# HGRN scan: q times f at the head, two more steps of projections behind the transposes, and the 16-token matmul behind the first level

## The chip, the cores and the metric

The kernel runs on one core of one Trainium2 chip. The metric is the device time of one execution in microseconds (us). A core has engines that each work through a queue of their own in order: PE (matmul, with PEld for its weight loads), VectorE (DVE), ScalarE (ACT), GpSimd (POOL), and SP, which here only issues transfers. They wait for each other through semaphores.

## The reference

The reference is one inference step of a hybrid decoder layer: a feed-forward half step, a mixer of two groups (HGRN2 with 4 heads of key and value size 128, and Mamba-2 with 8 heads of 64), one output projection, a second feed-forward half step and a norm. 1024 prompt tokens with 16 learned tokens ahead of them, and 8 single decoding tokens, share all weights. The part in question is the HGRN2 group. Per head, with f the forget gate, k = 1 - f, and a state S of 128x128:

```
S_t = diag(f_t) S_{t-1} + k_t v_t^T
o_t = S_t^T q_t
o   = rmsnorm_per_head(o) * hg_norm * silu(g)
```

Over a chunk of tokens this is computed as scores, decayed between the two positions, and a part from the state ahead of the chunk:

```
scores[t,s] = sum_k q[t,k] k[s,k] * prod_{s<j<=t} f[j,k]        (s <= t)
o[t]        = sum_s scores[t,s] v[s]  +  (q[t] * prod_{j<=t} f[j]) S_prev
```

## The kernel before

Tokens lie along the free dimension, channels on the 128 partitions; 1040 prompt tokens make 8 chunks of 128 and a rest of 16, and 8 decoding tokens stand behind them. The input projection is split in units of 128 output columns (q0, f0, v0, g0, q1, ... for the heads, z0 and z1 for the Mamba group), with three products for one fp32 product (`mm3`, L163 to L165, tiles `acc`).

*Projections as filling.* The class `Fill` is a generator over these units. One step, a call of `fill(1)`, is one `mm3`, three wide matmuls, and after eight steps a piece of 344 or 350 tokens is complete and is evacuated by ScalarE or VectorE (L1603, L1607 to L1610, L1561). The mixer's small matmuls wait for VectorE and ScalarE in many places, and `fill(n)` puts n steps of projection there. `fill.until(name)` runs steps until a unit is finished. The stock is fixed: steps taken earlier are missing later.

*Order.* In the mixer (in `body`) PE's order is that of the code, which a manual schedule keeps. The other engines, and the output projection that follows the mixer (`out_proj`, evacuated at L1850, weights split at L157 and L158), are put in order by a scheduler from its own estimates. A change of PE's order can so move rows on any engine, and matmuls of `out_proj` can stand ahead of the mixer's last ones.

*The scan* (`hgrn_scan`, once for each of the four heads; I call them first to fourth scan) goes like this. v is transposed on PE (L1650, L1653, L1654) and copied from PSUM by ScalarE (two copies L1651, then L1655, L1656, tiles `vt`, `vt8`, `vs8`). `fill(3)` follows. POOL zeroes `pp`, `p8` and `pd`; VectorE makes `qf` = q * f (L1686). PE makes the diagonal blocks k^T q of 32x32 (32 calls, 64 rows in the trace, L1696) and that of the last 16 tokens (L1697, into the bank `s8`). Then come seven levels of a tree, m = 1, 2, 4, ..., 64 (`LEVELS`): at each level 32 matmuls join the first half of every pair of m-token groups to the second (L1725 below m = 32, L1716 above), one more does it for the 16 tokens (L1737, into the same `s8`), VectorE scales the second halves of `qf` and the first halves of k by products of f (L1747, L1748), makes the next products of f (L1750), and copies the scores that count out of PSUM under a mask (L1700, L1701 for the diagonal, L1729, L1740 for a level). `fill(5)` closes each level. A level's matmuls read the `qf` and k that VectorE scaled in the level ahead. At m = 2 and m = 16 `samples` loads and advances four decoding states (L1669, L1670, L1673 to L1675). Banks of PSUM for all the mixer's small work come from one pool (`K.psm()`, tiles `mis`), and wide SBUF tiles from pools named by tag (`K.slot("s")`, `"u"`), so an allocation waits until the buffer's former readers are done.

*Around it.* `hgrn_out` squares the outputs, sums over channels on PE (L1828), takes the constant-scaled sums off PSUM (L1829) and calls `rstd_wide` for the inverse root: a table load and four activations on ScalarE (L199, L201), three wide operations on VectorE (L202, L203, L204), and then L1831. `ssm_norm` does the same for the Mamba group (L1576 to L1578, PE L1583, ScalarE L1584, `rstd_wide`, VectorE L1587 twice). `ssm_norm(0)` stands ahead of the second scan, `hgrn_out` of the second head ahead of the third, `ssm_norm(1)` behind the fourth. Three of the output projection's operands come back from DRAM (`split_spilled`, L2075 to L2077), one is split at the end of the block.

## Time and profile before

| | us |
|---|---|
| median of 3 runs | 1979.41 (1973.97, 1979.57, 1979.41) |
| profiled execution | 1973.32 |
| its span | 1971.5 |
| PE busy | 1923.6 |
| DVE busy | 1529.7 |
| ACT busy | 859.9 |
| first to fourth scan, start of the transposes | 917.58, 1009.04, 1063.05, 1130.80 |
| end of the last L1583 row | about 1181.4 |

Times within the trace are microseconds from the span's start. A row of the timeline has the start, the duration, the engine, the line, the operation, output and inputs by name, shapes and a count; in brackets stands the engine's idle time just before the row and what ended it. Matmuls overlap, so a row's duration is longer than the distance between two starts. In the list of waits a row names the engine and the waiting line, then what was waited for, the sum, the number of times and the longest. "issue" is a wait for nothing that the profile shows.

### The profile page before, as it was taken

To read this page: it belongs to the slowest core of one execution; us is meant where nothing else is said; L and a number is where in the kernel's file an instruction comes from. 1 tells how busy PE (TensorE), PEld (TensorE's weight loads), DVE (VectorE), ACT (ScalarE), POOL (GpSimd) and SP (SyncE) were. 2 spreads that over 40 slices of the span, in tenths; PEclk is the share of its full clock that TensorE was granted. 3 is DMA by queue.
4 is the path that set the end of the run, shared out by engine and by line. 5 is a ranking of instruction groups with operands and counts; after the bars stand their busy time and mean duration, and the time that the engine had idled before them with its cause. 6 is when DMAs were issued, how large, how long until landed. Compare 5 with 4: busy or idle time off the path is not lost.

```text
span 1971.5 us, 40943 instructions
## 1 busy us (share of the span) xinstructions
PE 1923.6 (98%) x16585; PEld 1885.4 (96%) x16585; DVE 1529.7 (78%) x2720; ACT 859.9 (44%) x1647; POOL 82.7 (4%) x135
## 2 busy tenths in 40 slices
PE   7999999999999999999999999999999999999997
PEld 6999999999999999998988989999999999999997
DVE  7788888888788776675755557888888888878973
ACT  7533232324534555465644535752332333354352
POOL 4000000000001310000000001200000000000000
PEclk9999999999999999999999999999999999999999
DMA  7233333335976632222522153224332333587851
GB/s 220 77 98 97 98 107 96 108 93 171 302 240 214 184 117 61 69 88 73 167 82 72 61 169 126 85 82 119 92 108 87 103 103 112 160 251 230 275 178 68
DMA packets 323877, 258.45 MB, mean 131 GB/s; under 512 B 17568, under 2 KB 299424, under 8 KB 323680
## 3 DMA queue, kind: packets, MB, share of 16 engines
q1 hardware_dynamic: 323448, 255.79, 42.1%
q8 instruction: 131, 2.15, 0.4%
q14 instruction: 58, 0.48, 0.1%
q0 software_dynamic: 224, 0.04, 0.0%
q10 hardware_dynamic: 16, 0.00, 0.0%
HBM read 190.79 MB, written 65.05 MB: 130 GB/s over the span
## 4 chain that ended last, share of the span: by engine, by line
PE 87%; DVE 7%; ACT 2%; DMA 2%; issue 1%; POOL 0%; SPq 0%; DVEq 0%; ACTq 0%; POOLq 0%
PE acc L163 26%; PE acc L165 26%; PE acc L164 26%; PE mis L163 1%; PE mis L165 1%; PE mis L164 1%; DVE u L352 1%; DMA s<-in_x_prompt_dram 1%; PE mis L1725 1%; PE mis L1449 0%; PE mis L1782 0%; DVE ws L466 0%; PE mis L1445 0%; DVE u L341 0%; DVE t L301 0%
## 5 line engine op out<-in xcount | busy, mean ns | idle before, releaser
L163 PE MATMUL acc<-u,ws 128*128 128x258 f32 (+3 forms) x4248 | 1242.9, 293 | 6.7 <-ACT t L674 1.7
L164 PE MATMUL acc<-u,ws 128*128 128x258 f32 (+3 forms) x4248 | 1232.1, 290 | 2.9 <-DVE u L352 2.7
L165 PE MATMUL acc<-u,ws 128*128 128x258 f32 (+3 forms) x4248 | 1231.1, 290 | 3.5 <-DVE ws L466 3.4
L163 PEld LDWEIGHTS acc<-u,ws 128*128 128x128 f32 x4248 | 803.9, 189 | 12.2 <-ACT t L674 2.1
L164 PEld LDWEIGHTS acc<-u,ws 128*128 128x128 f32 x4248 | 806.5, 190 | 5.8 <-DVE u L352 4.0
L165 PEld LDWEIGHTS acc<-u,ws 128*128 128x128 f32 x4248 | 803.6, 189 | 5.2 <-DVE ws L466 4.8
L466 DVE TENSOR_TENSOR ws<-r,ws 128x512 fp32r<-128x512 f32 x276 | 190.6, 691 | 75.0 <-ACT ws L462 74.9
L462 ACT CAST ws<-r 128x512 fp32r<-128x512 f32 x276 | 160.1, 614 | 13.3 <-ACT ws L462 7.8
L458 DVE TENSOR_TENSOR r<-r,r 128x512 f32<-128x512 f32 x176 | 121.5, 692 | 2.7 <-DMA r<-in_w_ffn_up_dram 1.2
L681 ACT ACTIVATE t<-t 128x516 f32<-128x516 f32 (+1 forms) x41 | 26.2, 639 | 212.9 <-DVE t L669 212.9
L712 ACT ACTIVATE t<-t 128x524 f32<-128x524 f32 (+1 forms) x47 | 29.9, 639 | 196.1 <-DVE t L669 196.1
L846 DVE TENSOR_TENSOR u<-u,u 128x1048 fp32r<-128x1048 f32 (+3 forms) x84 | 97.0, 1156 | 5.3 <-ACT u L842 4.5
L669 DVE TENSOR_TENSOR t<-t,u 128x524 f32<-128x524 f32 (+1 forms) x135 | 92.9, 697 | 2.8
L230 POOL TENSOR_TENSOR t<-t,t 128x262 f32<-128x262 f32 (+1 forms) x56 | 54.4, 981 | 823.6 <-ACT t L229 820.4
L158 DVE TENSOR_TENSOR ws<-r,ws 128x512 fp32r<-128x512 f32 x88 | 60.5, 698 | 36.0 <-ACT ws L157 35.6
L903 ACT CAST ws<-u 128x512 fp32r<-128x512 f32 (+1 forms) x72 | 42.2, 586 | 103.2 <-DVE u L898 100.2
L932 DVE SCALAR_TENSOR_TENSOR s<-acc,s 128x524 f32<-128x524 f32 (+3 forms) x88 | 54.6, 643 | 36.9 <-PE acc L165 36.5
L842 ACT CAST u<-u 128x1048 fp32r<-128x1048 f32 (+3 forms) x84 | 82.8, 988 | 0.0
L908 DVE TENSOR_TENSOR ws<-r,ws 128x512 fp32r<-128x512 f32 (+1 forms) x84 | 57.6, 693 | 22.3 <-ACT ws L903 22.2
L903 ACT CAST ws<-r 128x512 fp32r<-128x512 f32 (+1 forms) x84 | 47.9, 582 | 61.6 <-DVE r L898 37.0
L157 ACT CAST ws<-r 128x512 fp32r<-128x512 f32 x88 | 53.7, 618 | 35.6 <-PE acc L165 30.6
L908 DVE TENSOR_TENSOR ws<-u,ws 128x512 fp32r<-128x512 f32 (+1 forms) x72 | 47.4, 658 | 26.8 <-ACT ws L903 26.8
(417 smaller groups left out, 2297.9 us busy)
## 6 DMA issues: line engine op xcount, KB each, us to landing
r<-in_w_ffn_down_dram SPq DMA_DIRECT2D x128, 256.0 KB
hd<-s SPq DMA_DIRECT2D x93, 258.0 KB
r<-in_w_ffn_gate_dram SPq DMA_DIRECT2D x88, 256.0 KB
r<-in_w_ffn_up_dram SPq DMA_DIRECT2D x88, 256.0 KB
hd<-s SPq DMA_DIRECT2D x77, 262.0 KB
u<-hd SPq DMA_DIRECT2D x36, 516.0 KB
u<-hd SPq DMA_DIRECT2D x28, 524.0 KB
r<-in_w_in_dram SPq DMA_DIRECT2D x56, 256.0 KB
```

Of the source, the lines that this page charges most:

```text
L158: self.nc.vector.tensor_sub(lo, src, hi.bitcast(F32))
L163: mm(ps, whi, xhi, start=first, stop=False, skip_group_check=more)
L164: mm(ps, whi, xlo, start=False, stop=False, skip_group_check=more)
L165: mm(ps, wlo, xhi, start=False, stop=last, skip_group_check=more)
L458: self.K.nc.vector.tensor_tensor(self.raw[p], self.raw[x], self.raw[y], op)
L462: self.K.nc.scalar.copy(self.w[p][:, : self.n * P], self.raw[p])
L466: self.K.nc.vector.tensor_sub(t[:, 512 : 512 + w], self.raw[p], t[:, :w].bitcast(F32))
L669: nc.vector.tensor_mul(t, t if src is None else src, spread.lanes(i, cs))
L842: K.nc.scalar.copy(hi, lo.bitcast(F32))
L846: K.nc.vector.tensor_sub(lo, lo.bitcast(F32), hi.bitcast(F32))
L903: nc.scalar.copy(w[p, j, g][:, : n * P], src)
L908: nc.vector.tensor_sub(t[:, 512 : 512 + n * P], box[0], t[:, : n * P].bitcast(F32))
```

## The change

It has three parts, all in `hgrn_scan`:

- `qf` is allocated and made as the first thing in the function, ahead of the transposes (L1686 before, L1639 now).
- `fill(3)` behind the transposes becomes `fill(5)`: 15 wide matmuls, not 9.
- The bank `s8` is allocated, and the 16-token diagonal matmul is issued, behind the matmuls of the first level and not ahead of them (L1697 before, L1734 now).

```diff
     nc = K.nc
     q, f, kg, v = u["q"], u["f"], u["k"], u["v"]
+    qf = K.slot("s", w=TP)
+    nc.vector.tensor_mul(qf, q[:, :TP], f[:, :TP])
...
-    fill(3)
+    fill(5)
...
-    qf = K.slot("s", w=TP)
-    nc.vector.tensor_mul(qf, q[:, :TP], f[:, :TP])
...
-    s8 = K.psm()
     ps = K.psm()
     for c in range(8):
         for r in range(0, P, 32):
             cs = slice(P * c + r, P * c + r + 32)
             nc.tensor.matmul(ps[r : r + 32, 32 * c : 32 * c + 32], kg[:, cs], q[:, cs], start=True, stop=True)
-    nc.tensor.matmul(s8[:16, 64:80], kg[:, 1024:TP], q[:, 1024:TP], start=True, stop=True)
...
             copies.append(copy)
+        if li == 0:
+            s8 = K.psm()
+            nc.tensor.matmul(s8[:16, 64:80], kg[:, 1024:TP], q[:, 1024:TP], start=True, stop=True)
```

Line numbers shift by a few: L1650 to L1652 and L1651 to L1653 (transposes of v and their copies), L1696 to L1695 (diagonal), L1725 to L1722 and L1716 to L1713 (levels), L1700, L1701 to L1697, L1698, L1729 to L1726, L1673 to L1675; L1737, L1740, L1747, L1748 and L1750 keep theirs.

What it does to the order is seen at the start of the third scan. PE there, before: the last wide matmul behind the transposes, the diagonal blocks, the 16-token matmul, the first level, the next wide matmul. The semaphores waited for stand in brackets.

```order
L165 MATMUL acc_12682<-u_8461,ws_12433 128x344
L1696 MATMUL mis_12733<-u_11914,u_12032 32x32 [waits Activation_49]
L1696 MATMUL mis_12733<-u_11914,u_12032 32x32 x31
L1697 MATMUL mis_12732<-u_11914,u_12032 16x16 [waits DVE_49]
L1725 MATMUL mis_12767<-s_12728,u_12032 32x16 [waits DVE_49,Activation_49]
L1725 MATMUL mis_12767<-s_12728,u_12032 32x16 x31
L1737 MATMUL mis_12732<-s_12728,u_12032 16x8
L163 MATMUL acc_12682<-u_8462,ws_12433 128x344
```

And now:

```order
L165 MATMUL acc_12736<-u_8457,ws_12374 128x344
L1695 MATMUL mis_12746<-u_11914,u_12032 32x32 [waits Activation_49]
L1695 MATMUL mis_12746<-u_11914,u_12032 32x32 x31
L1722 MATMUL mis_12779<-s_12695,u_12032 32x16 [waits DVE_49,Activation_49]
L1722 MATMUL mis_12779<-s_12695,u_12032 32x16 x31
L1734 MATMUL mis_12812<-u_11914,u_12032 16x16 [waits Activation_49]
L1737 MATMUL mis_12812<-s_12695,u_12032 16x8
L163 MATMUL acc_12736<-u_8458,ws_12374 128x344
```

The 16-token matmul has moved behind the level, and it waits for ScalarE where it waited for VectorE. The wide matmuls belong to a later piece of the projection, since two more steps stand ahead. VectorE at the same place, before: the end of `hgrn_out`'s norm of the second head, with the product L1686 between L203 and L204.

```order
L202 TENSOR_TENSOR s_12633<-s_12633,s_12634 128x1032 [waits Activation_49]
L1700 COPY_PREDICATED t_12730<-mid,mis_12733 128x256 [waits PE_49,Pool_49]
L203 SCALAR_TENSOR_TENSOR s_12633<-s_12633,s_12634 128x1032 [waits DVE_49]
L1686 TENSOR_TENSOR s_12728<-u_11914,u_12031 128x1040 [waits Pool_49]
L204 SCALAR_TENSOR_TENSOR s_12634<-s_12633,s_12634 128x1032 [waits DVE_49]
L1747 TENSOR_TENSOR s_12728<-s_12728,u_12031 128x520 [waits DVE_49,PE_49]
L1831 TENSOR_TENSOR u_11403<-u_11403,s_12634 128x1032 [waits DVE_49]
L1748 TENSOR_TENSOR u_12032<-u_12032,u_12031 128x520
L1750 TENSOR_TENSOR s_12803<-u_12031 128x520
L1701 COPY_PREDICATED p_1598_12726<-mid,mis_12732 16x16 [waits Pool_49]
L1729 COPY_PREDICATED t_12730<-mask_8800,mis_12767 128x128
L1740 COPY_PREDICATED p_1598_12726<-mask_8800,mis_12732 16x8 [waits DVE_49]
```

And now:

```order
L1639 TENSOR_TENSOR s_12695<-u_11914,u_12031 128x1040
L1750 TENSOR_TENSOR s_12817<-u_12031 128x520
L202 TENSOR_TENSOR s_12639<-s_12639,s_12640 128x1032 [waits Activation_49]
L1697 COPY_PREDICATED t_12744<-mid,mis_12746 128x256 [waits PE_49,Pool_49]
L203 SCALAR_TENSOR_TENSOR s_12639<-s_12639,s_12640 128x1032 [waits DVE_49]
L1747 TENSOR_TENSOR s_12695<-s_12695,u_12031 128x520 [waits PE_49]
L204 SCALAR_TENSOR_TENSOR s_12640<-s_12639,s_12640 128x1032 [waits DVE_49]
L1748 TENSOR_TENSOR u_12032<-u_12032,u_12031 128x520
L1831 TENSOR_TENSOR u_11379<-u_11379,s_12640 128x1032 [waits DVE_49]
L1698 COPY_PREDICATED p_1600_12742<-mid,mis_12812 16x16 [waits Pool_49]
L1726 COPY_PREDICATED t_12744<-mask_8800,mis_12779 128x128
L1740 COPY_PREDICATED p_1600_12742<-mask_8800,mis_12812 16x8 [waits DVE_49]
```

The product and the first product of f (L1750) now stand ahead of L202, and L1748 ahead of L1831. On ScalarE the table load and one evacuation L1603, which stood between L201 and the two copies of v there, now stand ahead of L1829, so that the copies follow L201. In the second scan ScalarE's order is the same; on VectorE the product moves from behind L203 to ahead of L1578, and L1750 to between L203 and L204.

The second place is the end of the block, `ssm_norm(1)` behind the fourth scan. PE, before: the three matmuls L1583 in a row.

```order
L165 MATMUL acc_14071<-u_8463,ws_13454 128x344
L1583 MATMUL mis_14093<-s_14056,ones_83 128x344 [waits DVE_49]
L1583 MATMUL mis_14096<-s_14056,ones_83 128x344 [waits Activation_49]
L1583 MATMUL mis_14099<-s_14056,ones_83 128x344 [waits Activation_49]
L163 MATMUL acc_14071<-u_8464,ws_13454 128x344
```

And now, with tiles of `out_proj` (`acc_14200`, `acc_14214`) between them:

```order
L165 MATMUL acc_14097<-u_8457,ws_13449 128x344
L1583 MATMUL mis_14101<-s_14062,ones_83 128x344 [waits DVE_49]
L163 MATMUL acc_14200<-u_13513,ws_14192 128x258 [waits Activation_49]
...
L164 MATMUL acc_14200<-u_13925,ws_14197 128x258
L1583 MATMUL mis_14104<-s_14062,ones_83 128x344 [waits Activation_49]
L165 MATMUL acc_14200<-u_13924,ws_14197 128x258
L163 MATMUL acc_14200<-u_14143,ws_14197 128x258
L164 MATMUL acc_14200<-u_14144,ws_14197 128x258 [waits DVE_49]
L165 MATMUL acc_14200<-u_14143,ws_14197 128x258
L163 MATMUL acc_14214<-u_13513,ws_14192 128x258
L164 MATMUL acc_14214<-u_13514,ws_14192 128x258
L1583 MATMUL mis_14107<-s_14062,ones_83 128x344 [waits Activation_49]
L163 MATMUL acc_14097<-u_8458,ws_13449 128x344
```

Eight and six matmuls of `out_proj` stand between the three; in the order before its first one followed the first L1828, 28 rows later. From there on, and ahead of the first scan, the order is the same on every engine but for numbers.

## The prediction

> **What bounds the kernel now.** I read the page's busy line first.

> ```profile
> PE 1923.6 (98%) x16585; PEld 1885.4 (96%) x16585; DVE 1529.7 (78%) x2720; ACT 859.9 (44%) x1647; POOL 82.7 (4%) x135
> ```

> PE is busy for 98% of the span. The change takes no matmul away and adds none, so all it can win is time in which PE stands. The next view is that of PE's waits, from the first scan's transposes to behind the last `ssm_norm` (915 to 1205 us), the only stretch whose order changes.

> ```profile
> PE mis L1725 <- DVE s L1686: 3.5, 2, 2.1
> PE mis L1725 <- issue: 2.9, 2, 2.3
> PE mis L1583 <- ACT s L1584: 1.5, 2, 0.9
> PE mis L1697 <- ACT s L1651: 1.4, 1, 1.4
> PE mis L1725 <- DVE u L1748: 1.0, 2, 0.7
> PE mis L1697 <- DVE t L1700: 1.0, 1, 1.0
> PE mis L1737 <- DVE p L1740: 0.6, 1, 0.6
> ...
> ```

> These seven sum to 11.9 us. The waits on L1686 (qf) and the two of L1697 (5.9 us) lie in the second and third scan, and they are what the diff touches. The timeline of PE in the second scan shows their places: diagonal blocks, the 16-token matmul, the first level, wide products, the second level.

> ```profile
> 1011.67 0.76 PE L1696 MATMUL mis<-u,u 128*32 128x32 f32 x64
> 1013.88 0.21 PE L1697 MATMUL mis<-u,u 128*16 128x16 f32 x2 [1.45 <-ACT s L1651]
> 1015.42 1.05 PE L1725 MATMUL mis<-s,u 128*32 128x16 f32 x64 [1.32 <-DVE s L1686]
> ...
> 1019.62 0.33 PE L164 MATMUL acc<-u,ws 128*128 128x350 f32 x1
> 1019.79 0.32 PE L165 MATMUL acc<-u,ws 128*128 128x350 f32 x1
> 1020.44 0.73 PE L1725 MATMUL mis<-s,u 128*32 128x16 f32 x64 [0.32 <-DVE u L1748]
> 1021.81 0.21 PE L1737 MATMUL mis<-s,u 128*16 128x8 f32 x2 [0.64 <-DVE p L1740]
> ```

> **The two added steps.** A step is three wide matmuls, started 0.16 us apart (1019.62 to 1019.79), so two steps are six starts, 0.97 us. They come out of the same stock of projections, and the later `fill.until` finds them done. I take them as neutral in themselves: whatever stands behind them starts 0.97 us later in the scan, and 0.97 us less work is left for later. So a gain is the difference of two times at the end of a level, plus 0.97.

> **The second scan.** The timelines of VectorE and, in the last row, of ScalarE at the same place:

> ```profile
> 1011.62 1.23 DVE L202 TENSOR_TENSOR s<-s,s 128x1032 f32<-128x1032 f32 x1 [12.49 <-ACT s L201]
> ...
> 1014.04 1.23 DVE L1686 TENSOR_TENSOR s<-u,u 128x1040 f32<-128x1040 f32 x1
> 1015.19 1.23 DVE L204 SCALAR_TENSOR_TENSOR s<-s,s 128x1032 f32<-128x1032 f32 x1
> ...
> 1017.19 2.49 DVE L1587 SCALAR_TENSOR_TENSOR u<-u,col,s 128x1032 f32<-128x1032 f32 x2
> 1019.60 0.69 DVE L1748 TENSOR_TENSOR u<-u,u 128x520 f32<-128x520 f32 x1
> 1020.21 0.69 DVE L1750 TENSOR_TENSOR s<-u 128x520 f32<-128x520 f32 x1
> ...
> 1021.53 0.20 DVE L1740 COPY_PREDICATED p<-mask,mis 16x8 f32<-16x8 uint8 x1
> ```

> ```profile
> 1013.25 1.07 ACT L1651 COPY s<-mis 128x512 f32<-128x512 f32 x2
> ```

> The product now stands ahead of L202, where VectorE idles for 12.49 us (9.87 in the third scan), so its 1.23 us cost nothing; without that idle time they would delay L202 and all behind it. PE's diagonal starts at 1011.67 + 0.97 = 1012.64 and is done by 1013.4. The first level then needs only the first of the two copies of L1651, half of 1.07 us from 1013.25: about 1013.8. The 16-token matmul behind it needs the second copy, by then done. With 0.73 us of level and 15 wide matmuls (2.4 us) PE asks for the second level at about 1017.1. What is late next is the keys that L1748 scales. VectorE's queue up to there loses L1686 (1.15 from start to start) and takes in L1750 (0.61), which the new order puts ahead of L204: L1748 goes from 1019.60 to about 1018.85, with its end at 1019.5. PE waits 2.3 us there, counted to L1748's end. L1740 started 1.93 behind L1748, with L1750 (0.61) between them that now stands earlier: 1018.85 + 1.32, about 1020.2, done by 1020.35, and the level's last matmul (1021.81 before) starts then: 1.46 + 0.97 = 2.4 us won.

> What a wait costs beyond itself is seen in the stretches by time, whose columns are length, busy time of PE, PEld, DVE, ACT and POOL, then the granted clock.

> ```profile
> 929.90:933.30 3.40, 2.94 (x35) 2.91 (x36) 2.31 (x6) 1.59 (x5) 0.00 (x0) 0.50 0.64 178
> 1015.30:1018.70 3.40, 3.28 (x74) 3.28 (x75) 3.24 (x4) 0.60 (x1) 0.00 (x0) 0.50 0.35 87
> ...
> ```

> Behind the waits PE runs 3.4 us at clock 0.50. In the second scan the 15 wide matmuls then ended at 1019.79 + 0.16, 3.55 us after the level's end, where 2.4 would do: about 1.1 us. A standstill of 2.3 us may call the same, as the first scan's did (2.27 us, below). So 1.3 to 2.4; I take the middle, 1.85. [...]

> **The third scan**, from the timelines of PE, ScalarE and VectorE:

> ```profile
> 1065.64 0.76 PE L1696 MATMUL mis<-u,u 128*32 128x32 f32 x64
> ...
> 1069.74 0.94 PE L1725 MATMUL mis<-s,u 128*32 128x16 f32 x61 [2.15 <-DVE s L1686]
> ...
> 1074.96 0.17 PE L1737 MATMUL mis<-s,u 128*16 128x8 f32 x1
> ```

> ```profile
> 1064.38 1.33 ACT L201 ACTIVATE s<-s,lna 128x516 f32<-128x516 f32 x2
> ```

> ```profile
> 1065.74 1.23 DVE L202 TENSOR_TENSOR s<-s,s 128x1032 f32<-128x1032 f32 x1 [9.87 <-ACT s L201]
> ...
> 1071.45 1.23 DVE L1831 TENSOR_TENSOR u<-u,s 128x1032 f32<-128x1032 f32 x1
> ```

> Here the shifted end of a projection lets ScalarE evacuate it earlier, so both copies stand right behind L201: 1065.7 to 1066.8. The diagonal starts at 1066.6, the first level at about 1067.2 without a wait, the wide matmuls end at about 1070.4. VectorE does L202, L1697 behind the diagonal (an estimate of 0.3, as it is between L1740's 0.20 and L1750's 0.69), L203 (1.2), L1747 (0.6, its shape is that of L1748), L204 (1.2) and L1748 to about 1071.3, so the second level waits 0.9; L1831 (1.2) and three small copies (some 0.5, by L1740) stand ahead of its last matmul, which starts at about 1073.0, not 1074.96: 1.96 + 0.97 = 2.9. Two waits of about 1 us each may call the half clock, so 1.8 to 2.9, middle 2.35.

> **The first and the fourth scan** have no wait on the moved pieces; PE stands inside the 64 matmuls of a later level.

> ```profile
> 930.36 0.55 PE L1725 MATMUL mis<-s,u 128*32 128x16 f32 x25 [2.27 <-issue]
> ...
> 1144.65 0.38 PE L1725 MATMUL mis<-s,u 128*32 128x16 f32 x23 [0.72 <-DVE u L1748]
> 1145.67 0.52 PE L1725 MATMUL mis<-s,u 128*32 128x16 f32 x40 [0.65 <-issue]
> ```

> "Issue" means that nothing shown was waited for. In the DMA view of that standstill (927.8 to 930.4 us) the queue of instructions moves one block, among the loads of the data queue:

> ```profile
> q1 hardware_dynamic: 1171, 0.59, 82.8%
> q8 instruction: 1, 0.02, 2.7%
> ```

> I read it as PE waiting for its program. The first scan's loads are issued behind its copies, which don't move, while PE comes 0.97 later: between nothing and 0.97 us of the 2.27 go, if the block keeps its time; I take 0.5. For the fourth I take half of 0.72 + 0.65, 0.7, between 0 and 1.4. [...]

> **The tail.** The steps shift where `ssm_norm(1)` falls, and the new order puts 8 and 6 matmuls of `out_proj` between its three L1583. Rows of PE, then of ScalarE and VectorE:

> ```profile
> 1179.02 0.85 PE L1583 MATMUL mis<-s,ones 128*128 128x344 f32 x2 [0.91 <-ACT s L1584]
> 1180.50 0.85 PE L1583 MATMUL mis<-s,ones 128*128 128x344 f32 x2 [0.64 <-ACT s L1584]
> ```

> ```profile
> 1177.46 1.05 ACT L2076 CAST u<-u 128x1032 fp32r<-128x1032 f32 x1 [2.73 <-DMA u<-mspill]
> ```

> ```profile
> 1178.55 1.23 DVE L2077 TENSOR_TENSOR u<-u,u 128x1032 fp32r<-128x1032 f32 x1 [9.90 <-ACT u L2076]
> ```

> The 1.55 us of waits would be filled. But the eleventh of the 14 needs L2077, done at 1179.8, which hangs on a load that ScalarE already waits for, and the last L1828 will come before its L1829. Between nothing and 1.6; I take 0.8. The instructions that SP, POOL and the two other queues pass (weight loads one place earlier, some evacuations) I cost at nothing: PE's wait list shows none of them.

> **Sum.** 0.5 + 1.85 + 2.35 + 0.7 + 0.8 = 6.2 us. With the low ends (the first scan's block 0.5 later, so -0.5) 2.6, with the high ends 9.3. The profiled execution took 1973.32 us (span 1971.5 and 1.8 around it): 1967.1. The runs shown are at 1973.97, 1979.41 and 1979.57, so their median lies 6.1 above it. With the profiled one, the middle of four executions is 1976.7, and I subtract from that: 1970.5. A measurement tells about 0.3% from no change, 5.9 us, and the forecast stands just at that bound.

> **Rivals.** *All at the high end:* no half clock follows, the program comes in time, the tail fills: 9.3 us, 1967.4. For it speaks that the clock's stretches don't begin with a wait (929.9 lies inside one); against it that in both stretches shown a wait had just ended or was ending.
> *The wait only changes its name:* if VectorE's queue at the second level is longer than worked out, by the samples' products or a weight split, what L1686 gave back goes to L1748 and L1740: about 2 us in all, 1974.7. For it speaks that L1748 and L1740 already show 1.6 us of waits.
> *Slower: the program comes late.* The waits that go (5.9 us) are also time in which instructions arrive; diagonal, first level and 16-token matmul now follow each other without a pause, with loads beside them. Each standstill costs 2.27 and 1.1 of half clock, 3.4 us. Two undo the sum, and from four on (13.6 - 6.2 = 7.4 slower) the kernel is measurably slower, 1984. Against it: in the first and fourth scan these pieces already follow without a wait, and the stall came two levels later.

> **Chances.** Forecast 0.50, six tenths of it beyond 5.9 us (0.30 faster, 0.20 same); high end 0.15, faster; renamed 0.17, same; late program 0.18, slower. That is 0.45 faster, 0.37 same, 0.18 slower. The range reaches from the high end against the profiled execution (1973.3 - 9.3, rounded to 1963.5) to the upper run with nothing won and a little lost, 1981.

> **What would show it.** Rows of PE waiting for qf and for the 16-token matmul vanish; L1725's successor L1722 waits for L1748 about 2.3 us in the second scan and 0.9 in the third, and L1737 for L1740 about 1 in the third; L1583's waits go. Wrong I am if "issue" grows beyond 2.9 us, if clock 0.50 fills more stretches than before, or if PE stands at the first `out_proj` matmuls for the load of `mspill`.

## The result and the profile after

| | before | after |
|---|---|---|
| median of 22 runs each, us | 1979.39 (1973.78 to 1985.46) | 1971.87 (1969.89 to 1975.67) |
| ratio to before | | 0.997 [0.9963, 0.9978] |
| profiled execution, us | 1973.32 | 1971.54 |
| its span, us | 1971.5 | 1969.7 |

By the ratio the changed kernel is 5.9 us faster (4.4 to 7.3), just at the 0.3% that the prediction named as its bound; the two medians lie 7.5 us apart. The two profiled executions lie only 1.8 us apart, and why that is less is part of the answer. The busy line first.

```profile
PE 1926.6 (98%) x16585; PEld 1889.5 (96%) x16585; DVE 1531.6 (78%) x2720; ACT 861.8 (44%) x1648; POOL 81.8 (4%) x135
```

The number of matmuls is the same, and PE is still busy for 98%. PE's waits between 910 and 1205 us now are:

```profile
PE mis L1722 <- issue: 3.3, 4, 1.4
PE mis L1722 <- ACT r L1675: 2.4, 1, 2.4
PE acc L163 <- DVE s L1850: 1.6, 1, 1.6
PE mis L1722 <- DVE u L1748: 1.5, 2, 1.0
PE mis L1737 <- DVE p L1740: 0.8, 1, 0.8
PE mis L1722 <- ACT s L1653: 0.5, 1, 0.5
PE mis L1768 <- DVE u L1748: 0.2, 1, 0.2
```

The waits for qf (3.5 us), those of the 16-token matmul (2.4) and those of L1583 (1.5) are gone. What came in their place: one wait of 2.4 at a second level, 1.6 for L1850 in the tail, and 0.4 more of "issue". The list's sum went from 12.3 us (the seven rows that the prediction shows, and 0.4 for L1850) to 10.3. So the list alone does not show 5.9 us, and the stages have to be looked at. The timelines of PE and VectorE in the second scan:

```profile
1010.25 1.04 PE L1652 MATMUL mis<-ident,u 128*128 128x128 f32 x8
...
1013.86 0.76 PE L1695 MATMUL mis<-u,u 128*32 128x32 f32 x64
1015.11 0.70 PE L1722 MATMUL mis<-s,u 128*32 128x16 f32 x62 [0.49 <-ACT s L1653]
...
1020.87 0.73 PE L1722 MATMUL mis<-s,u 128*32 128x16 f32 x64 [2.38 <-ACT r L1675]
1021.63 0.21 PE L1737 MATMUL mis<-s,u 128*16 128x8 f32 x2
```

```profile
1012.84 1.23 DVE L202 TENSOR_TENSOR s<-s,s 128x1032 f32<-128x1032 f32 x1 [11.90 <-ACT s L201]
...
1017.62 2.49 DVE L1587 SCALAR_TENSOR_TENSOR u<-u,col,s 128x1032 f32<-128x1032 f32 x2
1020.03 0.69 DVE L1748 TENSOR_TENSOR u<-u,u 128x520 f32<-128x520 f32 x1
...
1021.37 0.20 DVE L1740 COPY_PREDICATED p<-mask,mis 16x8 f32<-16x8 uint8 x1
```

The second level starts 0.15 us behind the end of L1748 (1020.03 + 0.69). The list puts its wait down to L1675; in a second profile of the same kernel (below) it stands against L1748 with the same length. VectorE runs from L202 to L1740 without a pause, and PE stands until L1748 comes. From the transposes to the level's last matmul it is now 11.38 us (1010.25 to 1021.63), before 12.77 (1009.04 to 1021.81).

In the third scan:

```profile
1061.87 1.03 PE L1652 MATMUL mis<-ident,u 128*128 128x128 f32 x8
...
1065.41 0.76 PE L1695 MATMUL mis<-u,u 128*32 128x32 f32 x64
1066.02 0.69 PE L1722 MATMUL mis<-s,u 128*32 128x16 f32 x62
...
1070.36 0.73 PE L1722 MATMUL mis<-s,u 128*32 128x16 f32 x64 [0.99 <-DVE u L1748]
1071.85 0.21 PE L1737 MATMUL mis<-s,u 128*16 128x8 f32 x2 [0.77 <-DVE p L1740]
```

The first level follows the diagonal at once, and the two short waits at the second level are for L1748 and L1740. It is 9.98 us to the level's last matmul, against 11.91.

**Where the time went, stage by stage.** I took the distance from a scan's first transpose to the first L1768 (the transposes behind the last level), after minus before, less the 0.97 us of added work in it. The second column is the stretch to the next scan's transposes, with 0.97 us added for every two steps that are missing there: two in the first stretch, none in the second, four in the third, two in the tail. The tail runs from the fourth L1768 to a matmul that both orders share, at 1300 us.

| us, after minus before | levels | to the next scan |
|---|---|---|
| first scan | -1.82 | +1.62 |
| second | -1.74 | -1.62 |
| third | -2.36 | +1.52 |
| fourth | -0.21 | tail +0.92 |
| sum | -6.1 | +2.4 |

The levels won 6.1 us, and 2.4 were given back behind them. Both columns hold stretches of half clock. Of before they stood at 929.9, 1015.3, 1056.2 and 1069.9 us between 900 and 1200, three of the four inside the levels. Of after they stand at 962.3, 1105.7 and 1170.5, none inside the levels, each right behind the 16 one-column matmuls of L1811. These make the second column. In the first, PE's waits inside the levels went from 10.5 us to 8.5, so of the 6.1 us two are waits; what is left, four, goes with the three stretches of half clock. The stretches move between two executions of one kernel (a second profile of the changed one, below, has half clock from 1023.4, where this one has none), so this one pair of executions does not tell how much of the 6.1 belongs to the change; the runs of the experiments have to. Another 1.4 us were lost ahead of the first scan, where the order is the same, with half clock for 3.4 us at 20.3 and 6.8 us at 40.7, against one stretch of 3.4 at 42.5, and 0.5 us behind all of this. That is why these two executions differ by 1.8 us only.

### The profile page after: what moved, and what is told of

Same layout as the page of the kernel before. It is cut to its first block, busy times and chain, and to the rows that moved or that the text cites. A ratio compares the mean times of both kernels' runs of the same rounds, so it can differ in the third digit from the quotient of the medians.

```text
span 1969.7 us, 40941 instructions
## 1 busy us (share of the span) xinstructions
PE 1926.6 (98%) x16585; PEld 1889.5 (96%) x16585; DVE 1531.6 (78%) x2720; ACT 861.8 (44%) x1648; POOL 81.8 (4%) x135
## 3 DMA queue, kind: packets, MB, share of 16 engines
q8 instruction: 131, 2.15, 0.5%
## 4 chain that ended last, share of the span: by engine, by line
PE 83%; DVE 10%; ACT 2%; DMA 2%; issue 2%; SPq 0%; POOL 0%; DVEq 0%; ACTq 0%; POOLq 0%
PE acc L163 25%; PE acc L165 24%; PE acc L164 24%; PE mis L163 1%; PE mis L165 1%; PE mis L164 1%; DVE u L846 1%; DVE u L352 1%; DVE s L932 1%; DMA s<-in_x_prompt_dram 1%; DVE ws L908 1%; DMA r<-in_w_ffn_down_dram 1%; DVE ws L466 1%; DVE u L898 1%; PE mis L1449 0%
## 5 line engine op out<-in xcount | busy, mean ns | idle before, releaser
L164 PE MATMUL acc<-u,ws 128*128 128x258 f32 (+3 forms) x4248 | 1233.2, 290 | 2.7 <-DVE u L352 2.5
L165 PE MATMUL acc<-u,ws 128*128 128x258 f32 (+3 forms) x4248 | 1232.8, 290 | 2.8 <-DVE ws L466 2.7
L164 PEld LDWEIGHTS acc<-u,ws 128*128 128x128 f32 x4248 | 807.6, 190 | 5.2 <-DVE u L352 3.4
L165 PEld LDWEIGHTS acc<-u,ws 128*128 128x128 f32 x4248 | 804.7, 189 | 4.8 <-DVE ws L466 4.0
```

The source lines that it names most:

```text
L164: mm(ps, whi, xlo, start=False, stop=False, skip_group_check=more)
L165: mm(ps, wlo, xhi, start=False, stop=last, skip_group_check=more)
```

## The experiments

My theory at first was the prediction's: the gain is the waits on qf and on the 16-token matmul, which the moved product and the moved matmul take away, and the two steps cover what is late next. The rival was that the steps alone do it. Each part alone, then, and the whole once more.

**The product alone.**

```diff
+    qf = K.slot("s", w=TP)
+    nc.vector.tensor_mul(qf, q[:, :TP], f[:, :TP])
...
-    qf = K.slot("s", w=TP)
-    nc.vector.tensor_mul(qf, q[:, :TP], f[:, :TP])
```

> Only the product q times f moves to the head of the scan; three steps behind the transposes and the 16-token matmul ahead of the first level, as before. Theory (the wait on the product is the main cost): the waits of L1725 on the product (3.5 us) are gone, the wait of L1697 on the copy in the second scan (1.4 us) stays, and the second level waits about 2 us for L1748 in the second scan and 1 to 2 us in the third. Worked out: 1.46 us won in the second scan and 1.96 in the third, 3.4 us in all, and some half-clock stretches fewer; the tail is as before (1.5 us on L1584). Rival (the added steps give the gain): within 1 us of before.

Measured 1975.06 us, ratio 0.9991 [0.9978, 1.0004]: anything from 4.4 us faster to 0.8 slower, and no gain that can be told. In its one profiled execution the levels were 4.6 us shorter, counted as in the table, but only one stretch of half clock stood in them, against three, and the whole execution was 0.2 us shorter than that of before. So some gain may be in it, and it is not shown. Its waits:

```profile
PE mis L1697 <- ACT s L1653: 1.4, 1, 1.4
PE mis L1725 <- DVE p L1701: 1.4, 1, 1.4
...
PE mis L1697 <- DVE t L1700: 1.0, 1, 1.0
```

The wait on qf is gone. The 16-token matmul waits as before, and a second level now waits 1.4 us for VectorE's copy L1701.

**The two steps alone.**

```diff
-    fill(3)
+    fill(5)
```

> Only the two more steps behind the transposes. Theory: the first level of the second and third scan starts when the product is there, at the same time as before, with 0.97 us more of the projections done: 1.9 us won in the two scans, and 0.6 in the tail, where the interleaving of the output projection comes with these steps; 2.5 us in all. The waits on the product shrink from 3.5 to about 1.5 us and stay. Rival (the steps give the whole gain): 6 us or more.

Measured 1970.70 us, ratio 0.9967 [0.9955, 0.9979]: the whole gain of the change, from one line. My theory had given it far less. VectorE and PE's waits of this kernel show why. First VectorE in the third scan, then the list.

```profile
1064.22 1.23 DVE L202 TENSOR_TENSOR s<-s,s 128x1032 f32<-128x1032 f32 x1 [7.15 <-ACT s L201]
1065.37 0.69 DVE L1750 TENSOR_TENSOR s<-u 128x520 f32<-128x520 f32 x1
1065.98 1.23 DVE L203 SCALAR_TENSOR_TENSOR s<-s,s 128x1032 f32<-128x1032 f32 x1
```

```profile
PE mis L1737 <- DVE p L1740: 1.8, 2, 1.2
...
PE mis L1725 <- DVE s L1686: 1.3, 1, 1.3
```

The product L1686 is no longer behind L203. With the steps in front, the scheduler puts it ahead of L202 by itself, and the copies of v behind L201 too; only the second scan still waits for it. The line that reads as padding moved the other engines' work as well.

**The 16-token matmul alone.**

```diff
-    s8 = K.psm()
...
-    nc.tensor.matmul(s8[:16, 64:80], kg[:, 1024:TP], q[:, 1024:TP], start=True, stop=True)
...
+        if li == 0:
+            s8 = K.psm()
+            nc.tensor.matmul(s8[:16, 64:80], kg[:, 1024:TP], q[:, 1024:TP], start=True, stop=True)
```

> Only the 16-token matmul behind the first level. Theory: the first level still waits for the product (until about 1015.4 and 1069.7 us), so the waits on L1697 go over to L1722 whole: 2.4 us less there, 2.4 us more on the product, 0 won, within 1 us of before. Rival (the 16-token matmul is what held the queue): 2.4 us won.

Measured 1977.72 us, ratio 1.0004 [0.9994, 1.0014]: nothing. The wait changed its name whole:

```profile
PE mis L1722 <- DVE s L1686: 6.3, 2, 3.3
```

Before, L1686 and the two of L1697 were 5.9 us together.

**The changed kernel once more**, for a second profile and on the same chip as these three.

> The changed kernel once more, for a second profile beside the parts. The time ratio should be 0.997. [...]

Measured 1971.00 us, ratio 0.9965 [0.9954, 0.9975]. PE in its second scan:

```profile
1022.56 0.73 PE L1722 MATMUL mis<-s,u 128*32 128x16 f32 x64 [2.38 <-DVE u L1748]
1023.33 0.21 PE L1737 MATMUL mis<-s,u 128*16 128x8 f32 x2
1027.56 0.70 PE L1722 MATMUL mis<-s,u 128*32 128x16 f32 x62
```

The wait is the 2.38 of the first profile, now against L1748. But behind it PE went at half clock from 1023.4, and the third level comes 4.23 us after L1737 (1023.33 to 1027.56), where it came 2.74 after in the first profile (1021.63 to 1024.37). So 1.5 us of the 2.4 won at this place were lost again in this execution. The kernel with the steps alone goes another way to the same end:

```profile
1014.37 0.21 PE L1697 MATMUL mis<-u,u 128*16 128x16 f32 x2 [0.48 <-ACT s L1651]
1015.91 0.70 PE L1725 MATMUL mis<-s,u 128*32 128x16 f32 x62 [1.32 <-DVE s L1686]
...
1020.71 0.74 PE L1725 MATMUL mis<-s,u 128*32 128x16 f32 x64
```

It waits 0.48 and 1.32 ahead of the first level, runs at half clock from 1016.6, and comes to the second level just as L1748 is ready, with no wait there. Its half clock lies where PE would have waited anyway. The moved product turns two early waits into one late one, and nothing behind the late one hides the half clock. That is how I read it that the parts don't add; it rests on one execution of each kernel.

**The steps at another place.** Two more steps behind the levels, ahead of the output matmuls, and three behind the transposes as before: the stock of projections is shifted by as much, but nothing is covered.

```diff
-    fill(6)
+    fill(8)
```

> The kernel before, with the two more steps in another place: in the fill ahead of the output matmuls (six becomes eight), where PE waits for nothing, and three behind the transposes as before. The shift of the projection's pieces against the scans is the same, and with it the scheduler's order: in the third scan the product ahead of L202 and the copies of v behind L201, in the tail the output projection between the L1583. Theory A (the steps fill the wait behind the transposes, 0.97 us in each of two scans): the second scan is as before, the third wins some 1.8 to 3 us, the tail 0.6, in all 2.4 to 3.6 against about 4.4 in the trace of the steps alone; ratio 0.9980 to 0.9988. Theory B (the shift and the new order give it all): as the steps alone, ratio 0.9967. Theory C (only the place behind the transposes counts): within 1 us of before.

Measured 1977.74 us, ratio 0.999 [0.9979, 1.0001]. The interval leaves out the 0.9967 of the steps alone, so the place matters and the shift alone does not do it; a smaller gain, up to 4 us, it does not leave out. One row of PE in the third scan shows where it waits instead:

```profile
1075.20 0.21 PE L1737 MATMUL mis<-s,u 128*16 128x8 f32 x2 [2.93 <-DVE p L1740]
```

**Product and steps, the 16-token matmul in its old place.**

> The changed kernel without its third part: the 16-token matmul stands ahead of the first level again. Theory: the first level of the second scan starts about 0.5 us later, since it queues behind a matmul that waits for the second copy, and this is lost in the wait of the second level for L1748 (2.4 us there): no difference from the changed kernel within 0.5 us in the trace, ratio to before 0.9965 to 0.997. Rival (the third part is worth its own wait): 0.5 to 1.2 us slower than the changed kernel.

Measured 1971.46 us, ratio 0.9963 [0.9951, 0.9975]. The third part of the change is worth nothing, here as alone.

**The steps in the first scan alone, and in the second and third alone.**

```diff
-    fill(3)
+    fill((5, 3, 3, 3)[hd])
```

> The kernel before, with five steps behind the transposes of the first scan alone (5, 3, 3, 3 by head). In the profiles so far the 64 matmuls of the first scan's third level stand still for 1.2 to 2.3 us where three steps stand there, and for 0 to 1.2 us where five stand; with five, an output store comes ahead of one of the weight loads on SP, and the block of instructions comes sooner. Theory (the first scan is a third of the gain, by the instruction fetch): 1.5 to 2.5 us won in the first scan, none in the second and third, 1.5 to 3 in all, ratio 0.9985 to 0.9993. Rival (the first scan is worth 0.5 us, as predicted): within 1 us of before.

Measured 1975.75 us, ratio 0.999 [0.9979, 1.0002]. The other takes `(3, 5, 5, 3)`.

> The kernel before, with five steps in the second and third scan alone (3, 5, 5, 3 by head). Theory: the standstill in the first scan stays (1.2 to 2.3 us), the second wins about 1.2 and the third 1.5 to 2.5; 3 to 4 us in all, ratio 0.9980 to 0.9985. Rival (all of the gain comes from these two scans): ratio 0.9967.

Measured 1973.60 us, ratio 0.998 [0.9969, 0.9991]. By the ratios 2.0 and 4.0 us, which together is near the 6.5 of the steps in all scans. The 4.0 are clear of noise; the 2.0 of the first scan alone are not, since the interval takes in 1. The first scan's third level, in the kernel with the steps there and in the one without them:

```profile
932.29 0.84 PE L1725 MATMUL mis<-s,u 128*32 128x16 f32 x61 [1.54 <-DVE u L1748]
```

```profile
932.55 0.39 PE L1725 MATMUL mis<-s,u 128*32 128x16 f32 x25 [2.28 <-issue]
```

Without the steps the standstill of before (2.27) is back inside the 64 matmuls. With them PE waits ahead of the level for VectorE, and inside it there is none.

**More load on the data queue.** The steps alone, with two more transfers of 256 KB from SP ahead of the first scan's weight loads, which nothing reads.

```diff
+        if hd == 0 and b0 == 0:
+            for b in (0, 4):
+                dummy = K.dram.tile([P, 4, P], F32, name=K.uid("dummy"))
+                nc.sync.dma_start(dummy, vd[b : b + 4].partition_broadcast(P))
```

> The kernel with the two more steps alone, and two transfers of 256 KB that nobody needs, issued ahead of the weight loads in the first scan. Theory (the block of instructions waits among the loads): the standstill in the 64 matmuls of the third level comes back, 1 to 2.5 us put down to issue, with the block of the instruction queue moved 8 us or more behind the one ahead (7.0 without). Rival (the standstill has another cause in the program's order): no standstill there, or a wait for VectorE in its place.

Measured 1971.89 us, ratio 0.9972 [0.9962, 0.9982]. The lines are four further on here (L1729 is the level).

```profile
932.31 0.46 PE L1729 MATMUL mis<-s,u 128*32 128x16 f32 x33
932.99 0.41 PE L1729 MATMUL mis<-s,u 128*32 128x16 f32 x28 [0.22 <-issue]
```

The level falls into two pieces again, with 0.22 us between them, far less than the old 2.27. The block of the program went out 7.5 us behind the one before it, against 7.0 with the steps alone and 8.6 in the kernel before. That points the way the theory says, but two more transfers did not bring the long standstill back, as I had expected. What sets how late the block is stays open. The changed kernel itself shows 8.5 in its first profile, with 1.07 us of standstill, and 7.0 in its second, with none. And the kernel with five steps in the first scan alone shows 8.6 with no standstill: the block landed at 931.35, and the level, held up by VectorE, began only at 932.29. So I read it that the standstill hangs on whether PE comes to the end of a block before the next has landed; the last section has the times.

**Fewer half clocks?** The changed kernel, with one step of wide matmuls behind every second one-column matmul of L1811 (every scan), and three steps fewer in `ssm_norm(1)` and in `hgrn_out`. The question is whether half clock still follows these groups when they are spread, and what that is worth.

```diff
         nc.tensor.matmul(po8[:, 16 + b : 17 + b], states[b // 4 * 4][:, b % 4], qs[:, b : b + 1], start=True, stop=True)
+        if b % 2:
+            fill(1)
```

> The changed kernel with one step of projections behind every second of the eight matmuls of the decoding states (L1811, one column each), and three steps fewer behind them. In the six profiles so far a stretch of half clock followed 11 of 24 such groups of 16 rows, each time when all 16 lay in one window of 3.41 us; each such stretch made the next 15 wide matmuls about 1.4 us longer. [...]

Measured 1971.77 us, ratio 0.9963 [0.9951, 0.9975]. In its profile one of the four groups of L1811 is followed by half clock, where 20 of 52 were in the thirteen other profiles. The time is that of the changed kernel, so a gain from it is not shown.

**As many steps as each scan has use for.** VectorE's chain up to L1748 has its own length in each scan, so more steps in the second and third. The changed kernel with

```diff
-    fill(5)
+    fill((3, 10, 8, 3)[hd])
```

> The changed kernel with the steps behind the transposes set by head: 3, 10, 8, 3. If the waits that are left at the second level (2.4 us in the second scan; 1.1 and 0.9 in the third) are covered by more steps, 1.5 to 3 us come on top in these two scans, less the 0.6 of the tail, whose order falls back to that of before: 1 to 2.4 us faster than the changed kernel. Rival: VectorE's queue moves back with PE, since L1747 now stands behind L1587 there, and nothing is won.

Measured 1971.34 us, ratio 0.9953 [0.9938, 0.9968]. With the first scan at 3, its standstill is back (1.9 us of "issue"). So five there:

```diff
-    fill(5)
+    fill((5, 10, 8, 3)[hd])
```

> The changed kernel with 5, 10, 8, 3 steps behind the transposes by head. Against the kernel with 3, 10, 8, 3 the first scan should lose its standstill (some 2 us won), so about 2 us faster than that one and 3 faster than the changed kernel: ratio to before 0.994 to 0.995. Rival: the tail, whose three L1583 stand in a row again, and the half clock take it back, and the ratio is that of the changed kernel, 0.9965.

Measured 1966.81 us (1966.13 to 1967.68), ratio 0.9945 [0.9933, 0.9956]: 10.9 us faster than the kernel before, and by the ratios (0.9970 and 0.9965) 4 to 5 us better than the changed one. These are five runs, and the interval just touches that of the changed kernel's second measurement. Its waits above 1 us:

```profile
PE mis L1722 <- DVE u L1748: 3.4, 2, 2.3
PE mis L1722 <- ACT r L1675: 1.7, 1, 1.7
PE mis L1583 <- ACT s L1584: 1.4, 2, 0.8
```

"issue" is not in its list at all, and the levels of the second and third scan are 3.8 and 4.0 us shorter than before, counted as in the table above. The first scan's standstill is gone as expected, but not its time: its levels were 0.5 us longer than before, with a wait of 2.3 us for L1748 at the third level and half clock at 933.8. So the 2 us expected there are not seen in this execution.

## Why the prediction was right, and where it was not

The forecast of 1970.5 lies 1.4 us from the median measured, and the sum of 6.2 us by the measured 5.9 of the ratio. Part of that closeness is luck. The 1976.7 that the prediction subtracted from lies 2.7 us below the median of the 22 runs, and the medians differ by 1.3 more than its sum. Its terms stand less well than the sum, too: one was too small and three too large. The column on the right holds what the levels of a scan won, against the one profile of before, in every single execution of a kernel with five steps there (the changed kernel twice, the steps alone, product and steps, and others). Each figure so includes the half clock that happened to stand in that execution, and in that of before.

| term | predicted | measured |
|---|---|---|
| first scan | 0.5 (-0.5 to 0.97) | -0.5 to 2.5 (eight executions, six of them 1.5 to 2.5) |
| second scan | 1.85 (1.3 to 2.4) | 0.9 to 1.7 (seven) |
| third scan | 2.35 (1.8 to 2.9) | 1.3 to 2.8 (seven) |
| fourth scan | 0.7 | 0.0 to 0.3 (six) |
| tail | 0.8 | 0.7 (one, with no half clock in it), -1.2 to -0.5 (four, with half clock) |

- **Second scan, its mechanism: right.** PE waits for L1748, 2.4 us where 2.3 was said, and the level's last matmul comes 1.39 + 0.97 = 2.36 us sooner; 2.4 was worked out. The half clock behind that wait came in the second profile and not in the first: the two cases between which I took the middle. It is no even chance, though: of the seven executions with five steps there, six show half clock in this scan's levels, and the low end of 1.3 was nearer than the middle. (The working moves L1748 by 0.75 us and names 1.15 less 0.61; the 0.16 that VectorE itself waited ahead of L1747 goes unnamed. Against L202 it moved by 0.79.) In the first profile 0.6 us went elsewhere, since PE stood 0.48 of "issue" in a later level:

```profile
1032.10 0.26 PE L1722 MATMUL mis<-s,u 128*32 128x16 f32 x9 [0.48 <-issue]
...
1078.85 0.21 PE L1722 MATMUL mis<-s,u 128*32 128x16 f32 x3 [0.40 <-issue]
```

- **Third scan, its mechanism: right.** No wait at the first level, 0.99 for L1748 (0.9 said), 0.77 for L1740 (1 said); 1.93 + 0.97 = 2.90 us at the level's last matmul, 2.9 worked out. The second row above is what it lost later. No half clock followed the two short waits in the first profile.
- **First scan: mis-sized, since its half clock was left out.** "Between nothing and 0.97 us of the 2.27 go, if the block keeps its time". In the first profile it kept its time: it went out 10.36 us behind the scan's first transpose, 10.34 before. The standstill fell from 2.27 to 1.07 us, and 0.55 of waiting for L1748 came ahead of it, so 0.65 us less waiting, within the range given. The rest of the 1.8 us won is the half clock at 929.9, which is gone; the prediction shows that stretch and puts no price on it here. In the second profile the block went out 8.60 us behind the transpose, and there is no standstill. Half clock stood in this scan's levels in five of six profiles with three steps there and in two of eight with five; those two are the executions that won 0.2 us and lost 0.5.

```profile
930.32 0.45 PE L1722 MATMUL mis<-s,u 128*32 128x16 f32 x33 [0.55 <-DVE u L1748]
931.84 0.41 PE L1722 MATMUL mis<-s,u 128*32 128x16 f32 x28 [1.07 <-issue]
```

- **Fourth scan: no gain.** The wait on L1748 went, and a standstill of 1.38 us came at an earlier level, against one of 0.65 before. All six executions with five steps in this scan have one of 1.3 to 1.6 us there. The prediction's sum had no term for a standstill that the steps bring with them; only its rival *the program comes late* named one.
- **Tail: the waits went, another came.** L1583 has no wait. But PE, ahead by as much, now meets VectorE's queue at the evacuation of `out_proj`. The rows of PE, then of VectorE:

```profile
1193.40 0.39 PE L163 MATMUL acc<-u,ws 128*128 128x258 f32 x1 [1.61 <-DVE s L1850]
```

```profile
1189.33 2.49 DVE L1587 SCALAR_TENSOR_TENSOR u<-u,col,s 128x1032 f32<-128x1032 f32 x2
1191.78 1.23 DVE L202 TENSOR_TENSOR u<-u,u 128x1032 f32<-128x1032 f32 x1
1192.92 0.42 DVE L1850 TENSOR_TENSOR s<-s,acc 128x258 f32<-128x258 f32 x1
```

The first L1850 starts at 1192.92, behind L1587 and L202, and PE has no bank until it is done. It started at 1193.09 before, where PE came later and waited 0.36. The prediction named the wrong thing to be late next, the load of `mspill`; that was in time. The +0.92 of the table's tail holds the half clock at 1170.5, which alone made the wide matmuls behind it 1.5 us late.

**The attribution was wrong where the sum was right.** I put the second and third scan's gain down to the product and the moved matmul, with the steps neutral "in themselves". The steps alone bring 0.9967; the product alone can't be told from nothing, the product on top of the steps adds nothing (0.9963 with it), and the moved matmul is nothing. In the second and third scan, what bounds PE up to the second level is VectorE's chain from L202 to L1748 and L1740. PE arrives there too early, and only work that fills the time helps; an earlier operand ahead of it lengthens the wait behind it.

Of the rivals, *the wait only changes its name* describes the product alone and the 16-token matmul alone, but not the whole. *The program comes late* fell: "issue" was 3.3 us in the first profile, just over the 2.9 I had set as a sign, and 1.3 in the second; the longest standstill fell from 2.3 to 1.4 and 1.3. Between 900 and 1200 us half clock filled three stretches in the first profile and five in the second, against four, so that sign of being wrong shows nothing either way. *All at the high end* had the place of the first scan right, and no more.

**How much is clock.** Over 32 runs of the kernel before, the time falls by 1.1 us for each 0.001 of mean granted clock. That clock's mean was 0.9911 in these runs, and 0.9931 in the 12 of the changed kernel beside them. As an estimate from that slope, about 2 us of the gain are then fewer half clocks. The waits can be counted directly: PE's waits between 910 and 1205 us sum to 12.3 us before, to 10.3 and 9.2 in the changed kernel's two profiles, and to 9.2 to 10.1 in four other kernels with five steps in every scan. That is 2 to 3 us. About 1 us of the 5.9 neither count places. The runs of before spread over 11.7 us, those of after over 5.8.

## What to carry to other kernels

Where one engine waits for a chain on another, ask first how long that chain is and put independent work of that length in front of the wait; making one operand earlier only moves the wait, as the product alone and the 16-token matmul alone did. How much each place can take differs, and steps sized by scan brought 4 to 5 us more than the change did. And try a change's parts alone before giving each a price: a line that seems to add only filling can reorder the other engines too.

## What was not expected of the hardware

**Half clock behind a stretch in which PE is busy.** The prediction saw half clock behind standstills of about 2 us. The stretches by time show a second kind; the first two rows are the changed kernel around L1811 (its columns as in the prediction), the third a standstill.

```profile
1102.30:1105.70 3.40, 3.40 (x30) 3.25 (x30) 1.34 (x2) 0.60 (x1) 1.27 (x3) 1.00 0.99 380
1105.70:1109.10 3.40, 3.40 (x13) 3.40 (x13) 1.06 (x3) 1.10 (x4) 0.00 (x0) 0.50 0.04 17
...
1016.90:1020.30 3.40, 1.59 (x10) 1.30 (x9) 3.40 (x5) 1.04 (x3) 0.00 (x0) 1.00 0.46 125
1020.30:1023.70 3.40, 2.79 (x78) 2.70 (x79) 3.40 (x11) 1.80 (x5) 0.00 (x0) 1.00 1.04 378
```

And of the kernel with the steps alone:

```profile
1013.20:1016.60 3.40, 1.60 (x134) 1.39 (x133) 3.37 (x4) 3.16 (x7) 0.00 (x0) 1.00 0.01 1
1016.60:1020.00 3.40, 3.40 (x18) 3.40 (x13) 3.40 (x5) 0.99 (x3) 0.00 (x0) 0.50 0.40 99
```

**Standstills inside a group of small matmuls.** PE stood 0.22 to 2.28 us between two matmuls of one level, with nothing shown that it waited for, while a block of its program was under way among loads. The traces show what goes with it. The fourteen profiles have 28 such waits on "issue" between 60 and 1960 us. Each ended 1.2 to 1.6 us after a block of the instruction queue q8 had landed: before at 929.03 and 930.36 (landed, PE goes on), in the changed kernel at 930.45 and 931.84. And counted in PE's rows (matmuls, weight loads and the semaphore rows of its queue), all 28 stand at whole multiples of 256 rows from each other, give or take one (14786 and 19905 before; 14785, 17089, 18370 and 19649 in the changed kernel), while q8 brings 131 blocks for 33,530 rows, one for every 256. I read it that PE had come to the end of one block and the next was not there. At none of some 1,800 such places did PE pass sooner than 1.0 us after the landing (of 129 each in the profiles of before and after, at the least 1.04 and 1.28). It stood at 28 of them. What makes a block late is not shown: added load moved it by half a microsecond only.
